# Conditional second scatters, shorter gathers and another row order of w_down in a 32-expert layer

## Chip, cores and metric

The kernel runs on one core of a Trainium2 chip. The metric is the device time of one execution in microseconds (us), lower is better.

## The reference

One decoder layer on x of shape 512 x 1024, float32: a mixing sublayer of three token mixers with an output projection and a LayerNorm, and then the part that this change touches, a routed feed-forward sublayer of 32 experts, of which each token uses 4:

```python
logits = (xt @ router_w + router_b).astype(F32)
top_val, top_idx = lax.top_k(logits, TOP_K)          # 4 of 32
gate = jax.nn.softmax(top_val, axis=-1)
...
gu = xb @ w_gu[e] + b_gu[e]                          # rows of expert e, 1024 x 2048
glu = jnp.minimum(gu[:, :D_FF], SWIGLU_LIMIT)
lin = jnp.clip(gu[:, D_FF:], -SWIGLU_LIMIT, SWIGLU_LIMIT)
act = glu * jax.nn.sigmoid(SWIGLU_ALPHA * glu) * (lin + 1.0)
return act @ w_dn[e] + b_dn[e]                       # 1024 x 1024
...
y_sorted = out[dest] * gate.reshape(-1)[order][:, None].astype(h.dtype)
y = jnp.zeros_like(xt).at[tok_sorted].add(y_sorted)
h = layer_norm(DEEPNORM_ALPHA * h + ffn, ln2_g[l], ln2_b[l])
```

So 512 x 4 = 2048 rows are spread over 32 experts, and each expert's weights (8 MB of w_gate_up and 4 MB of w_down in float32) are read once.

## The kernel before

The first 380 us hold the mixing sublayer. Then `experts` (line 1338) walks over the 32 experts. An expert has room for 96 slots (`CAP`); slots 0 to 63 are the low ones, 64 to 95 the high ones. Slots that no token fills are padding slots: their index in the table `gidx` points to one of 128 spare rows of zeros behind the 512 token rows of the DRAM buffer `hd`, and their row in `sidx` points to spare rows of the DRAM buffer `yd`.

For expert e the program does this:

- `load_gu` and `load_dn` (lines 1175 and 1183) issue eight loads of 1 MB of w_gate_up and four of 1 MB of w_down on SP's queue, through `load` (line 1171). They go into a ring of 18 buffers (`chunk`, tile `wc`), so a load waits until the load 18 places earlier has been used, and SP also waits for older loads to land. One partition of a w_gate_up load is one row of 8 KB; one partition of a w_down load is two rows of 4 KB that lie 128 rows apart.
- `expert_gather` (line 1191) issues on POOL an indirect DMA that reads 96 rows of 4 KB from `hd` into the tile `xg`, two experts ahead. `expert_xT` (line 1200) transposes them on PE (line 1206) and copies them with ACT.
- `gu_low` (line 1263) multiplies the low slots with w_gate_up, `gu_high` (line 1269) the high slots. The high part stands in a branch (`past64`, line 1256): `fill` (line 1249) reads the expert's count into a register of PE, and PE skips the part when the count is 64 or less. Experts 0 and 31 always take it.
- `swiglu` and `swiglu_T` (lines 1274 and 1287) apply the activation on DVE and ACT and transpose the result on PE in blocks of 128 columns.
- `dn` (line 1297) multiplies with w_down, one expert later: the low slots into the PSUM bank `p0`, the high slots into `p2`, these again in PE's branch. Then, for every expert but the last, ACT scales both banks with the gates (line 1329) and POOL issues two indirect DMAs that add into `yd` (line 1330): 128 rows of 2 KB for the low slots and 128 rows of 1 KB for the high slots, whether or not the high slots hold anything. The last expert's output goes another way, in `tail`.

A scheduler orders the instructions of each engine; a branch is moved only as a whole. After the last expert, `overflow` handles experts with more than 96 rows (a branch that is not taken here), and `tail` adds `yd` and applies the LayerNorm.

Of the kernel before, what the change touches and what calls it, by code (L numbers as in the profile page):

```python
# [24 lines left out]
F32 = mybir.dt.float32  # L25
# [4 lines left out]
AF = mybir.ActivationFunctionType  # L30
OP = mybir.AluOpType
# [4 lines left out]
T, D, NT, NK = 512, 1024, 4, 8  # L36
NE, FF = 32, 1024
KAPPA = math.exp(-0.5)
ALPHA = 2.0 ** 0.25
CAP = 96  # L40
# [86 lines left out]
class Trunk:  # L127
# [1055 lines left out]
    def load_dn(self, e):  # L1183
        out = []
        for k in range(0, NK, 2):
            w, gate = self.chunk()
            self.load(w.rearrange("p (k c) -> p k c", k=2), self.a["w_down"][e, k * 128:(k + 2) * 128].rearrange("(k p) c -> p k c", p=128), gate)
            out += [w[:, 0:1024], w[:, 1024:2048]]
        return out

    def expert_gather(self, e):
        x = self.mw.tile([128, D], F32, name="xg", bufs=2)
        self.nc.gpsimd.indirect_dma_start(out=x[0:CAP], out_offset=None, in_=self.hd,  # L1193
                                          in_offset=bass.IndirectOffsetOnAxis(ap=self.gidx[:, e:e + 1], axis=0))
        return x

    def tbank(self):
# [51 lines left out]
    def fill(self, e):  # L1249
        if e in (0, NE - 1):  # L1250
            return None
        return self.nc.values_load(self.cnti[0:1, e:e + 1], engines=[mybir.EngineType.PE], min_val=0, max_val=T,
                                   skip_runtime_bounds_check_because="a count of rows, which only decides a branch")


# [31 lines left out]
    def swiglu_T(self, t):  # L1287
        nc = self.nc
        aT = self.mw.tile([128, 6, 128], F32, name="aT")
        for z0, n in ((0, 4), (4, 2)):  # L1290
            p = self.tbank()
            for z in range(n):
                nc.tensor.transpose(p[:, z * 128:z * 128 + 128], t[:, (z0 + z) * 128:(z0 + z) * 128 + 128], self.ident)
            nc.scalar.activation(aT[:, z0:z0 + n], p[:, 0:128 * n].rearrange("p (z t) -> p z t", z=n), AF.Copy)  # L1294
        return aT

    def dn(self, e, aT, wd, n):
        nc, mm = self.nc, self.nc.tensor.matmul
        p0 = self.mps.tile([128, 512], F32, name="dn0")
        if e == 0:  # L1300
            self.dn2 = self.mps.tile([128, 512], F32, name="dn2")[:, 0:256]
        p2 = self.dn2

        def high():
            for k in range(NK):
                for c in range(4):
                    mm(p2[32 * c:32 * c + 32], aT[:, 4 + k % 2, 32 * (k // 2):32 * (k // 2) + 32], wd[k][:, 256 * c:256 * c + 256],  # L1307
                       start=(k == 0), stop=(k == NK - 1), skip_group_check=True)

        for k in range(NK):  # L1310
            for h in range(2):
                mm(p0[64 * h:64 * h + 64], aT[:, k % 4, 64 * (k // 4):64 * (k // 4) + 64], wd[k][:, 512 * h:512 * h + 512], start=(k == 0), stop=(k == NK - 1))  # L1312
        self.past64(n, high)
        if e == NE - 1:
            his = []
            for g, p in enumerate((p0, p2)):
                hi, lo = self.slast[2 * g:2 * g + 2]
                his.append(nc.scalar.activation(hi, p, AF.Copy, scale=self.gate[:, g, e:e + 1]))
                nc.vector.scalar_tensor_tensor(lo, p, self.gate[:, g, e:e + 1], hi, OP.mult, OP.subtract)
            self.warm = self.mw.tile([128, 1], F32, name="warm")  # L1320
            w = nc.scalar.activation(self.warm, self.eps[1e-5], AF.Sqrt)
            for h in his:
                self.after(w, h)
            return
        sts = []
        for g, p in enumerate((p0, p2)):
            n = 512 >> g
            o = self.mw.tile([128, n], F32, name=f"eo{g}")
            nc.scalar.activation(o, p, AF.Copy, scale=self.gate[:, g, e:e + 1])  # L1329
            sts.append(nc.gpsimd.indirect_dma_start(out=self.yd.rearrange("t (c f) -> (t c) f", f=n),  # L1330
                                                    out_offset=bass.IndirectOffsetOnAxis(ap=self.sidx[:, g, e:e + 1], axis=0),
                                                    in_=o, in_offset=None, compute_op=OP.add))
        self.tc.declare_no_dep(sts[1].ins, sts[0].ins, reason="rows of other slots")
        if self.added is not None:
            self.after(sts[1], self.added, mybir.DependencyClass.Sync)
        self.added = sts[0]

    def experts(self):
        xs, xT = {}, {0: self.first_xT()}
        wg, pend, self.added = self.load_gu(0), None, None  # L1340
        self.route_slots()
        for e in range(NE):
            w = wg
            t, sel = xT.pop(e)
            n = self.fill(e)
            p = self.gu(t, sel)
            for k in range(NK):
                self.gu_low(p, k, t, w[k])
                if k % 4 == 3:
                    self.past64(n, lambda: [self.gu_high(p, z, t, w[z]) for z in range(k - 3, k + 1)])  # L1350
                if e == 0:
                    if k == 0:
                        self.route_counts()
                        self.route_table()
                        self.tables()
                        xs[1] = self.expert_gather(1)
                    elif k < 5:
                        self.out_init(k - 1)
                if k == 3:
                    if e + 1 < NE:  # L1360
                        wg = self.load_gu(e + 1)
                    wd = self.load_dn(e)
                    if e + 2 < NE:
                        xs[e + 2] = self.expert_gather(e + 2)
                if k == (6 if e == 0 else 3) and e + 1 < NE:
                    xT[e + 1] = self.expert_xT(e + 1, xs.pop(e + 1))
            a = self.swiglu(p)
            if e == NE - 1:
                self.tail_setup()
                aT = self.swiglu_T(a)  # L1370
            if pend:
                self.dn(*pend)
            if e == NE - 1:
                self.tail_rows()
            pend = (e, aT if e == NE - 1 else self.swiglu_T(a), wd, n)
        self.dn(*pend)
# [290 lines left out]
```

## Time and profile before

| | us |
|---|---|
| median of 3 runs (lowest, highest) | 1513.34 (1508.01, 1516.6) |
| the profiled execution, its own time | 1505.45 |
| span of that execution, first to last instruction | 1503.7 |
| PE busy over the span | 1339.4 |
| DVE, ACT, POOL busy over the span | 464.9, 298.9, 251.3 |
| mean granted TensorE clock, as a share of full speed | 0.968 |

The profiled execution took 1.75 us more than its span. It is 0.5% below the median of the runs. "Busy" is the time in which an engine executes instructions; waits, branches and the issuing of DMAs are not in it. In the rows below an arrow names what ended an idle time, PEld is PE's loading of stationary operands, and q1 is the hardware queue of SP's loads, q0 the software queue of POOL's indirect DMAs.

### The profile page before, as it was taken

How to read it: one execution, taken by the hardware profiler on the slowest of the kernel's cores; microseconds unless marked ns; L12 is line 12 of the kernel's file. 1: busy time of each engine (PE TensorE's matmuls, PEld its weight loads, DVE VectorE, ACT ScalarE, POOL GpSimd, SP SyncE). 2: the span in 40 equal slices, each digit the busy share in tenths (PEclk: the TensorE clock that was granted, in tenths of full speed). 3: DMA queues.
4: the chain of work that ended last, by engine and by line, in shares of the span. 5: the costliest groups of instructions: out<-in, count | busy, mean ns of one | idle time of the engine just before them, and what ended most of it. 6: DMA issues, size and time to landing. Idle time of an engine off the chain costs nothing. (4 is left out here: it accounts for less than half of the span.)

```text
span 1503.7 us, 19610 instructions
## 1 busy us (share of the span) xinstructions
PE 1339.4 (89%) x7852; PEld 623.5 (41%) x7853; DVE 464.9 (31%) x1108; ACT 298.9 (20%) x628; POOL 251.3 (17%) x221
## 2 busy tenths in 40 slices
PE   7899979998899998987899999999888888899993
PEld 5577878875533432322223333333222222333322
DVE  4767687888621121111111121111111111111115
ACT  4444343443111111111111111111111110111103
POOL 1211227232201111111111111111111111110111
PEclk9999997999999999999999999999999999999996
DMA  7222233446699999999999999999999999999984
GB/s 252 65 56 70 49 75 101 140 143 236 251 377 393 382 392 392 392 387 387 395 393 395 393 394 395 394 388 393 390 388 395 395 396 394 395 394 406 401 284 131
DMA packets 114059, 467.94 MB, mean 311 GB/s; under 512 B 17412, under 2 KB 28196, under 8 KB 81178
## 3 DMA queue, kind: packets, MB, share of 16 engines
q1 hardware_dynamic: 96058, 434.57, 74.1%
q0 software_dynamic: 13328, 27.63, 8.3%
q10 hardware_dynamic: 4560, 4.15, 0.9%
q8 instruction: 82, 1.34, 0.4%
q14 instruction: 31, 0.25, 0.0%
HBM read 445.97 MB, written 20.33 MB: 310 GB/s over the span
## 5 line engine op out<-in xcount | busy, mean ns | idle before, releaser
L1267 PE MATMUL gu<-wc,xT 128*64 128x512 f32 x2048 | 491.4, 608 | 85.6 <-DMA wc<-w_gate_up 82.8
L1267 PEld LDWEIGHTS gu<-wc,xT 128*64 128x64 f32 x2048 | 140.3, 138 | 420.0 <-issue 233.0
L1280 DVE TENSOR_SCALAR glu<-gu 128x256 f32<-128x256 f32 (+1 forms) x64 | 35.6, 556 | 865.3 <-PEq L1260 398.6
L1312 PE MATMUL dn<-wc,aT 128*64 128x512 f32 x1024 | 247.7, 603 | 3.5 <-PEq L1260 2.1
L1281 ACT ACTIVATE glu<-glu 128x256 f32<-128x256 f32 (+1 forms) x64 | 33.5, 524 | 574.0 <-DVE glu L1280 573.8
L1193 POOL DMA_INDIRECT xg<-hd,gidx x31 | 29.5, 952 | 668.9 <-PE tr L1206 656.4
L1330 POOL DMA_INDIRECT yd<-eo,sidx x62 | 96.4, 1555 | 267.6 <-ACT eo L1329 267.1
L1312 PEld LDWEIGHTS dn<-wc,aT 128*64 128x64 f32 x1024 | 65.5, 136 | 117.3 <-issue 101.6
L1272 PE MATMUL gu<-wc,xT 128*32 128x512 f32 x960 | 111.3, 596 | 0.0
L222 PE MATMUL pi<-xhi,whi 128*128 128x512 f32 x152 | 63.4, 417 | 8.8 <-ACT whi L172 8.8
L1329 ACT ACTIVATE eo<-dn,gate 128x512 f32<-128x512 f32 (+1 forms) x62 | 36.0, 581 | 167.7 <-PE dn L1307 78.1
L223 PE MATMUL pi<-xlo,whi 128*128 128x512 f32 x152 | 63.0, 414 | 0.8 <-DVE xlo L173 0.6
L1207 ACT ACTIVATE xT<-tr 128x384 f32<-128x384 f32 x62 | 29.9, 491 | 167.0 <-PE tr L1206 167.0
L173 POOL TENSOR_TENSOR wlo<-wraw,whi 128x512 fp32r<-128x512 f32 (+1 forms) x28 | 39.8, 1425 | 135.0 <-ACT whi L172 132.4
L224 PE MATMUL pi<-xhi,wlo 128*128 128x512 f32 x152 | 61.1, 402 | 0.0
L1272 PEld LDWEIGHTS gu<-wc,xT 128*32 128x32 f32 x960 | 27.7, 109 | 79.2 <-issue 79.2
L1307 PE MATMUL dn<-wc,aT 128*32 128x256 f32 x960 | 56.1, 381 | 1.0 <-ACT aT L1294 1.0
L172 ACT ACTIVATE whi<-wraw 128x512 fp32r<-128x512 f32 (+1 forms) x54 | 33.9, 631 | 54.1 <-DMA wraw<-w_in 27.0
L1307 PEld LDWEIGHTS dn<-wc,aT 128*32 128x32 f32 x960 | 29.5, 110 | 33.4 <-issue 14.0
L1283 DVE SCALAR_TENSOR_TENSOR glu<-glu 128x256 f32<-128x256 f32 (+1 forms) x64 | 35.6, 556 | 7.7 <-ACT glu L1281 6.9
L222 PEld LDWEIGHTS pi<-xhi,whi 128*128 128x128 f32 x152 | 29.4, 193 | 18.1 <-ACT whi L172 8.5
L1282 DVE TENSOR_SCALAR glu<-gu 128x256 f32<-128x256 f32 (+1 forms) x64 | 35.3, 551 | 3.0 <-PE gu L1267 3.0
(488 smaller groups left out, 1544.0 us busy)
## 6 DMA issues: line engine op xcount, KB each, us to landing
wc<-w_gate_up SPq DMA_DIRECT2D x256, 1024.0 KB
wc<-w_down SPq DMA_DIRECT2D x128, 1024.0 KB
wraw<-w_in SPq DMA_DIRECT2D x46, 256.0 KB
wraw<-w_out SPq DMA_DIRECT2D x16, 256.0 KB
xraw<-xT SPq DMA_DIRECT2D x4, 512.0 KB
res<-x SPq DMA_DIRECT2D x4, 512.0 KB
hd<-res ACTq DMA_DIRECT2D x4, 512.0 KB
res<-yd POOLq DMA_DIRECT2D x4, 512.0 KB
```

What stands on the lines that cost most here:

```text
L173: return (eng or nc.vector).tensor_tensor(lo, src, hi, OP.subtract)
L222: nc.tensor.matmul(p, hi, xh, start=(k == 0), stop=False)
L223: nc.tensor.matmul(p, hi, xl, start=False, stop=False)
L224: nc.tensor.matmul(p, lo, xh, start=False, stop=(k == NK - 1))
L1267: mm(p[q][64 * h:64 * h + 64], xT[:, k, 0:64], w[:, 1024 * q + 512 * h:1024 * q + 512 * h + 512], start=False, stop=(k == NK - 1))
L1272: self.nc.tensor.matmul(p[2][32 * c:32 * c + 32], xT[:, k, 64:96], w4[:, c], start=False, stop=(k == NK - 1), skip_group_check=True)
L1280: nc.vector.tensor_scalar(out[:, c], g, 7.0, None, OP.min)
L1283: nc.vector.scalar_tensor_tensor(out[:, c], ln[:, c], 1.0, out[:, c], OP.add, OP.mult)
L1307: mm(p2[32 * c:32 * c + 32], aT[:, 4 + k % 2, 32 * (k // 2):32 * (k // 2) + 32], wd[k][:, 256 * c:256 * c + 256], start=(k == 0), stop=(k ...
L1312: mm(p0[64 * h:64 * h + 64], aT[:, k % 4, 64 * (k // 4):64 * (k // 4) + 64], wd[k][:, 512 * h:512 * h + 512], start=(k == 0), stop=(k == N ...
L1329: nc.scalar.activation(o, p, AF.Copy, scale=self.gate[:, g, e:e + 1])
L1330: sts.append(nc.gpsimd.indirect_dma_start(out=self.yd.rearrange("t (c f) -> (t c) f", f=n), out_offset=bass.IndirectOffsetOnAxis(ap=self.s ...
```

## The change

Three things change. The low slots' output is scaled and scattered as soon as the low matmuls are done; the scaling and the scatter of the high slots move into the branch that holds their matmuls, so the count is now loaded into registers of ACT and POOL too, and these two engines branch as PE does. The gather gets a bounds check: indices over 511, which are those of the padding slots, are not fetched, so `xg` becomes two fixed tiles that are set to zero once at the start of `experts`. And a load of w_down puts two neighbouring rows (8 KB in one piece) in one partition; to match, the transposes after SwiGLU take every second column of a block of 256 instead of 128 neighbouring columns.

```diff
--- before.py
+++ after.py
@@ -1184,14 +1184,15 @@
         out = []
         for k in range(0, NK, 2):
             w, gate = self.chunk()
-            self.load(w.rearrange("p (k c) -> p k c", k=2), self.a["w_down"][e, k * 128:(k + 2) * 128].rearrange("(k p) c -> p k c", p=128), gate)
+            self.load(w.rearrange("p (k c) -> p k c", k=2), self.a["w_down"][e, k * 128:(k + 2) * 128].rearrange("(p k) c -> p k c", k=2), gate)
             out += [w[:, 0:1024], w[:, 1024:2048]]
         return out
 
     def expert_gather(self, e):
-        x = self.mw.tile([128, D], F32, name="xg", bufs=2)
+        x = self.xg[e % 2]
         self.nc.gpsimd.indirect_dma_start(out=x[0:CAP], out_offset=None, in_=self.hd,
-                                          in_offset=bass.IndirectOffsetOnAxis(ap=self.gidx[:, e:e + 1], axis=0))
+                                          in_offset=bass.IndirectOffsetOnAxis(ap=self.gidx[:, e:e + 1], axis=0),
+                                          bounds_check=T - 1, oob_is_err=False)
         return x
 
     def tbank(self):
@@ -1249,7 +1250,7 @@
     def fill(self, e):
         if e in (0, NE - 1):
             return None
-        return self.nc.values_load(self.cnti[0:1, e:e + 1], engines=[mybir.EngineType.PE], min_val=0, max_val=T,
+        return self.nc.values_load(self.cnti[0:1, e:e + 1], engines=[mybir.EngineType.PE, mybir.EngineType.Activation, mybir.EngineType.Pool], min_val=0, max_val=T,
                                    skip_runtime_bounds_check_because="a count of rows, which only decides a branch")
 
 
@@ -1287,10 +1288,11 @@
     def swiglu_T(self, t):
         nc = self.nc
         aT = self.mw.tile([128, 6, 128], F32, name="aT")
+        t2 = t.rearrange("q (c p z) -> q c z p", z=2, p=128)
         for z0, n in ((0, 4), (4, 2)):
             p = self.tbank()
             for z in range(n):
-                nc.tensor.transpose(p[:, z * 128:z * 128 + 128], t[:, (z0 + z) * 128:(z0 + z) * 128 + 128], self.ident)
+                nc.tensor.transpose(p[:, z * 128:z * 128 + 128], t2[:, (z0 + z) // 2, z % 2], self.ident)
             nc.scalar.activation(aT[:, z0:z0 + n], p[:, 0:128 * n].rearrange("p (z t) -> p z t", z=n), AF.Copy)
         return aT
 
@@ -1310,7 +1312,28 @@
         for k in range(NK):
             for h in range(2):
                 mm(p0[64 * h:64 * h + 64], aT[:, k % 4, 64 * (k // 4):64 * (k // 4) + 64], wd[k][:, 512 * h:512 * h + 512], start=(k == 0), stop=(k == NK - 1))
-        self.past64(n, high)
+        def out(g, p):
+            w = 512 >> g
+            o = self.mw.tile([128, w], F32, name=f"eo{g}")
+            nc.scalar.activation(o, p, AF.Copy, scale=self.gate[:, g, e:e + 1])
+            return nc.gpsimd.indirect_dma_start(out=self.yd.rearrange("t (c f) -> (t c) f", f=w),
+                                                out_offset=bass.IndirectOffsetOnAxis(ap=self.sidx[:, g, e:e + 1], axis=0),
+                                                in_=o, in_offset=None, compute_op=OP.add)
+
+        if e < NE - 1:
+            first = out(0, p0)
+
+        def past():
+            high()
+            if e < NE - 1:
+                second = out(1, p2)
+                self.tc.declare_no_dep(second.ins, first.ins, reason="rows of other slots")
+                if self.added is not None:
+                    self.after(second, self.added, mybir.DependencyClass.Sync)
+
+        self.past64(n, past)
+        if e < NE - 1:
+            self.added = first
         if e == NE - 1:
             his = []
             for g, p in enumerate((p0, p2)):
@@ -1321,21 +1344,11 @@
             w = nc.scalar.activation(self.warm, self.eps[1e-5], AF.Sqrt)
             for h in his:
                 self.after(w, h)
-            return
-        sts = []
-        for g, p in enumerate((p0, p2)):
-            n = 512 >> g
-            o = self.mw.tile([128, n], F32, name=f"eo{g}")
-            nc.scalar.activation(o, p, AF.Copy, scale=self.gate[:, g, e:e + 1])
-            sts.append(nc.gpsimd.indirect_dma_start(out=self.yd.rearrange("t (c f) -> (t c) f", f=n),
-                                                    out_offset=bass.IndirectOffsetOnAxis(ap=self.sidx[:, g, e:e + 1], axis=0),
-                                                    in_=o, in_offset=None, compute_op=OP.add))
-        self.tc.declare_no_dep(sts[1].ins, sts[0].ins, reason="rows of other slots")
-        if self.added is not None:
-            self.after(sts[1], self.added, mybir.DependencyClass.Sync)
-        self.added = sts[0]
 
     def experts(self):
+        self.xg = [self.mw.tile([128, D], F32, name=f"xg{q}") for q in range(2)]
+        for x in self.xg:
+            self.nc.gpsimd.memset(x[0:CAP], 0.0)
         xs, xT = {}, {0: self.first_xT()}
         wg, pend, self.added = self.load_gu(0), None, None
         self.route_slots()
```

## Rows read from the trace of the kernel before

**Rows 1.** The page's slices: what the DMA engines moved, 40 slices of 37.6 us

```profile
GB/s 252 65 56 70 49 75 101 140 143 236 251 377 393 382 392 392 392 387 387 395 393 395 393 394 395 394 388 393 390 388 395 395 396 394 395 394 406 401 284 131
```

**Rows 2.** Windows, three stretches: length, busy (instructions) of each engine, PEclk, DMA share, GB/s

```profile
434.00:570.00 136.00, 134.53 (x758) 51.87 (x756) 21.01 (x46) 20.07 (x41) 20.90 (x16) 1.00 1.03 390
570.00:1318.00 748.00, 664.59 (x3718) 218.28 (x3718) 94.37 (x220) 85.08 (x172) 86.64 (x65) 0.99 1.03 393
1318.00:1454.00 136.00, 132.41 (x824) 42.61 (x813) 19.32 (x40) 14.33 (x29) 14.08 (x10) 1.00 1.01 392
```

**Rows 3.** Waits of PE, 570 to 1318 us: total, times, longest

```profile
PE gu L1267 <- DMA wc<-w_gate_up: 79.7, 84, 2.7
```

**Rows 4.** Timeline of SP's queue: start, length, loads of w_gate_up; first and last periods

```profile
579.34 18.25 SPq L1171 DMA_DIRECT2D wc<-w_gate_up  x8
...
1334.18 17.94 SPq L1171 DMA_DIRECT2D wc<-w_gate_up  x8
...
1366.13 18.07 SPq L1171 DMA_DIRECT2D wc<-w_gate_up  x8
```

**Rows 5.** Windows of 6 and 3.5 us: weights alone, then beside a gather

```profile
1106.00:1112.00 6.00, 5.78 (x32) 2.36 (x30) 0.00 (x0) 1.01 (x3) 0.95 (x1) 1.00 1.02 418
1114.20:1117.70 3.50, 1.94 (x8) 0.48 (x8) 0.00 (x0) 1.45 (x3) 1.62 (x2) 1.00 1.04 318
```

**Rows 6.** DMA queues in 1114.2:1117.7 (gather): packets, MB, share of 16 engines

```profile
q1 hardware_dynamic: 100, 0.72, 67.3%
q0 software_dynamic: 93, 0.38, 34.7%
q8 instruction: 1, 0.02, 2.1%
```

**Rows 7.** DMA queues in 1118.4:1121.6, the scatter of 1 KB rows

```profile
q1 hardware_dynamic: 136, 1.00, 78.0%
q0 software_dynamic: 133, 0.13, 25.5%
```

**Rows 8.** DMA queues in 1121.6:1125.6, the scatter of 2 KB rows

```profile
q1 hardware_dynamic: 159, 1.16, 71.4%
q0 software_dynamic: 157, 0.26, 35.8%
```

**Rows 9.** DMA packets in 690:694 (w_down alone) and in 1352:1360 (w_gate_up alone)

```profile
DMA packets 430, 1.64 MB, mean 410 GB/s; under 512 B 30, under 2 KB 30, under 8 KB 430
...
DMA packets 460, 3.36 MB, mean 420 GB/s; under 512 B 51, under 2 KB 51, under 8 KB 51
```

**Rows 10.** The page's groups: the experts' matmuls, two instructions for each call

```profile
L1267 PE MATMUL gu<-wc,xT 128*64 128x512 f32 x2048 | 491.4, 608 | 85.6 <-DMA wc<-w_gate_up 82.8
...
L1272 PE MATMUL gu<-wc,xT 128*32 128x512 f32 x960 | 111.3, 596 | 0.0
...
L1307 PE MATMUL dn<-wc,aT 128*32 128x256 f32 x960 | 56.1, 381 | 1.0 <-ACT aT L1294 1.0
```

**Rows 11.** Lines 1260 and 1252, PE's sequencer: duration ns min/median/max, first and last start

```profile
L1260 PEldq COMPARE_BRANCH  x129: 65/179/369, 426.4 to 1448.3; - x129
...
L1252 PEldq TENSOR_LOAD <-cnti x30: 297/306/482, 425.8 to 1393.2; - x30
```

**Rows 12.** Timeline of POOL: one expert's gather and scatters, idle time before each

```profile
1110.19 0.95 POOL L1193 DMA_INDIRECT xg<-hd,gidx  x1 [24.82 <-PE tr L1206]
1112.72 1.56 POOL L1330 DMA_INDIRECT yd<-eo,sidx  x1 [1.58 <-ACT eo L1329]
1115.17 1.55 POOL L1330 DMA_INDIRECT yd<-eo,sidx  x1 [0.90 <-ACT eo L1329]
1147.69 0.95 POOL L1193 DMA_INDIRECT xg<-hd,gidx  x1 [30.97 <-PE tr L1206]
```

**Rows 13.** Line 1293, the transposes after SwiGLU: duration ns min/median/max

```profile
L1293 PEld LDWEIGHTS tr<-ident,glu x192: 137/140/143, 424.8 to 1448.0; 128*128 128x128 f32 x192
```

**Rows 14.** POOL around the start of the experts: groups, and its timeline

```profile
L688 POOL MEMSET ba<- 96x1024 f32 x1 | 0.9, 948 | 8.1 <-PE ps L652 8.1
...
391.84 2.58 POOL L1097 TENSOR_TENSOR ohv<-ohv,ro 128x512 f32<-128x512 f32 x1 [9.13 <-DVE ohv L1098]
```

## The prediction

> **What bounds the kernel now.** I read the page's slices first: from the twelfth slice to the thirty-eighth the DMA engines move 377 to 406 GB/s without a break [rows 1], and this is the walk over the experts. Then I asked for windows of that stage. In three stretches of four, twenty-two and four experts the DMA share is 1.03, 1.03 and 1.01, so the sixteen engines are never idle; PE is busy for 134.5 of 136 us, 664.6 of 748 us and 132.4 of 136 us [rows 2]. So in the middle stretch PE has 748 - 664.6 = 83.4 us of idle time, and the waits name its cause: 79.7 us for loads of w_gate_up [rows 3]. In the first and last stretch the two are nearly in balance, with 1.5 and 3.6 us of PE idle. The reader is to see that the DMA engines set the pace of the middle stretch, that a microsecond taken from their work there is a microsecond of the kernel until PE's idle time is used up, and that at both ends PE leaves little to win.
>
> One period is seen in SP's timeline: 22 experts from 579.34 to 1334.18 us, 34.3 us each; the next, which holds no gather since the last expert's rows are already there, takes 1366.13 - 1334.18 = 31.95 us [rows 4]. An expert's weights are 12 MB in units of 1,048,576 bytes, 12.58 million bytes; at the 418 GB/s of undisturbed weights [rows 5] they need 30.1 us. So the gather and the two scatters cost about 4.2 us of DMA time per expert, 1.9 us of it scatters and 2.4 us the gather.
>
> **The change part by part.** DMA time first, as a loss: the length of a window, less the time that the weights moved in it would need alone.
>
> Gather: in 3.5 us only 0.72 + 0.02 million bytes of weights and instructions move [rows 6], 1.77 us worth at 418, so it costs 1.73 us. The share stays at 1.04 while the rate falls to 318 GB/s [rows 5], so no engine waits: the packets get slower, those of the weights too. The gather's own packets take 34.7% of 3.5 us, 1.21 us; the other 0.5 us is slowing of its neighbours. Of 31 x 96 = 2976 gathered rows, 2048 less expert 0's own (65 to 96, as it takes the branch with no row beyond 96) are real, so a third is padding. No row of this trace shows a gather with rows left out. The saving per gather lies between nothing (if the skipped rows, which stand together at the end, belong to a few of the sixteen engines while the others carry theirs as before; a load has landed only when its slowest part has) and a third of the 2.4 us that the periods give, 0.8 us. I take a third of the packets' own time, 0.40 us, since that time is what the row shows to belong to the rows themselves.
>
> Scatter of the high slots: 3.2 us with 1.00 million bytes of weights, 2.39 us worth, so 0.81 us [rows 7]; its packets' time, 25.5% of 3.2, is 0.82 us too. (The low slots' scatter costs 4 - 1.16 / 0.418 = 1.22 us by [rows 8]; the three together are 3.8 us beside the 4.2 us of the periods.) How many vanish: the low gate-up matmuls are 2048 for 32 experts, 64 each; the high ones are 960, again 64 for each expert that takes the branch, so 15 do, experts 0 and 31 among them [rows 10], and 17 skip both matmuls now and scatter in the future. By the order of PE's branches 12 of the 17 scatters fall in the middle stretch, 3 before it and 2 after.
>
> w_down: where it is alone on the engines they move 410 GB/s, where w_gate_up is alone 420 GB/s [rows 9]. 4.19 million bytes take 10.23 and 9.99 us, so 8 KB rows save 0.24 us per expert; the lower bound is nothing, since mixed stretches run at 418. I take 0.24. The Trainium skill, "DMA: Bandwidth & Descriptors", section "Why small descriptors are slow (HBM only)", gives each packet a fixed overhead of about 3 cycles beside one for each 32 bytes: worked out from its figures, an estimate of 131 against 129.5 cycles for 4 KB, 1.1%, or 0.11 us per expert. Our rows show 2.4%; by the page the forecast would be 3 us later, so nothing hangs on it.
>
> What is added. ACT and POOL load a count and branch for 30 experts. PE does so already: 0.31 us for a load, 0.18 us at the median and 0.37 us at most for a branch [rows 11]. I cost it at nothing, because POOL idles 25 to 31 us before each gather [rows 12] and ACT is busy for 85 of 748 us [rows 2]; uncovered it would be 30 x 0.5 = 15 us. On ACT the scaling of the high slots now waits inside the branch for PE's high matmuls, with the next copies to `xT` and `aT` queued behind it; on POOL the scatter waits for that scaling, with the gather two experts ahead behind it. The gather has a whole period in hand, so neither moves PE unless the order on ACT changes (a rival below). The low scatter leaves a few us earlier, which changes no amount of DMA work. The transposes now load every second column: a load takes 140 ns [rows 13]; the bounds are 0 and double that, 192 x 0.14 = 27 us of PE over the stage if none of it overlapped; I take 0, since loads run beside matmuls, and the middle stretch would cover its share, 18 us, in PE's idle time. The bounds check lengthens a POOL instruction at most, in the same idle time. Setting `xg` to zero is twice the 0.95 us of a 96 x 1024 memset, in the 9.1 us that POOL waits before line 1097 [rows 14]; it may disturb DVE's routing there, bounds 0 and 2 us, and I take 1 us. Skipping ACT's scaling 17 times frees an engine that bounds nothing.
>
> **The sum.** Middle stretch: 12 x 0.81 + 22 x 0.40 + 22 x 0.24 = 9.7 + 8.8 + 5.3 = 23.8 us, well below PE's 83.4 us of idle. First stretch: 3 x 0.81 + 4 x 0.40 + 4 x 0.24 = 5.0 us less DMA work, of which I count PE's idle 1.5 us. Last stretch: 2 x 0.81 + 4 x 0.24 = 2.6 us, within PE's 3.6 us. Less 1 us for the start: 23.8 + 1.5 + 2.6 - 1 = 26.9 us, say 27. Against the profiled execution 1505.45 - 27 = 1478.4 us. The runs' median lies 7.9 us above that execution, so for the median I forecast 1513.3 - 27 = 1486 us.
>
> **The rivals.** (1) The skipped rows and the longer rows save nothing: only the scatters count, 27 - 8.8 - 5.3 = 13 us, 1500 us. For it: the weights' packets suffer beside a gather as long as any engine still carries it. Against it: packets' own time falls with their number. (2) The gather's cost falls by a full third of what the periods show: 22 x 0.4 = 9 us more, 1477 us, and still within PE's idle time. (3) PE takes over as the bound, by added work or waits of d us per expert: the transposes' loads double without overlap (27 / 32 = 0.85 us), and ACT's branch holds copies up. The middle stretch hides 22 d up to 83 - 24 = 59 us, the eight experts at the ends hide nothing. At 0.85 us 7 us are lost and 20 us of gain remain; at 2.5 us, 20 us, and the time is 1506 us, no change that can be told. (4) Slower: the branch blocks of ACT, the same sum with a larger d. Were the copies to `xT` ordered behind the block, PE would stand between two experts until the high matmuls and the scaling are done and the copies made, or until the skip is signalled. The price is at most the 56.1 / 15 = 3.7 us of high matmuls [rows 10] and two copies, some 4 to 5 us per expert. At 3 us the middle loses 66 - 59 = 7 and the ends 24 us, 1517 us; so it decides from about 3 us, and at 4 us it gives 1486 + 29 + 32 = 1547 us. Against it: PE has branched so all along, and the copies to `xT` need the transposes alone, not the scaling. The Trainium skill, "Runtime: NRT & Kernel Launch", section "Instruction fetch mechanics", says that a taken branch out of the prefetched window stalls on a fetch, which would feed this rival; 129 branches on PE with none above 0.37 us [rows 11] do not show it.
>
> **How the numbers follow.** The forecast's case, 20 to 34 us gained, gets 0.50; rival 1, 10 to 20 us, 0.20; rival 2, above 34 us, 0.10; rival 3 with a gain under 8 us, 0.12; rival 4, 0.08. A measurement of this kernel can tell about 0.5%, 7.6 us, from no change. So faster 0.80, same 0.12, slower 0.08. The range: all terms at their upper bounds give 1470 us (22 x 0.4 = 9 us for the gather, 3.5 us of the first stretch's lost gain and 1 us at the start, with 2 us for the runs' own spread), the lower ones 27 - 14 - 1 for the start - 3 for transposes at the ends = 9 us of gain, 1504 us. 1470 to 1504 us leaves out about 2 in 10, mostly rivals 3 and 4.
>
> **What would show it.** In the profile after: 45 instead of 62 scatters; some 990 fewer packets of 4 KB in the software queue, and w_down's 8 KB packets; periods of about 33 us; windows beside a gather that are shorter, not just emptier; the DMA share still about 1.03 in the middle stretch with PE idle near 60 us. The prediction is wrong if that share falls below 1 (PE or a wait has taken over), if PE's waits name ACT's copies or branches, or if a gather still costs 1.7 us.

## The result and the profile after

The changed kernel takes 1492.94 us (median of 4 runs, 1488.69 to 1493.81), the kernel before 1511.91 us on the same chip (one run more than the three ahead of the prediction); the ratio is 0.9878 [0.9855, 0.9901], 18 to 19 us less. The profiled execution took 1492.41 us with a span of 1490.7 us, 13.0 us below the span of before.

Windows of the middle and the last stretch of the changed kernel, as in [rows 2] (length, busy time of PE, PEld, DVE, ACT and POOL, granted clock, DMA share, GB/s):

```profile
570.00:1318.00 748.00, 680.77 (x3850) 230.22 (x3850) 94.39 (x220) 83.28 (x168) 74.64 (x56) 0.99 1.02 396
...
1318.00:1454.00 136.00, 132.97 (x820) 43.15 (x812) 19.37 (x41) 13.60 (x27) 14.59 (x13) 1.00 0.92 356
```

PE's idle time in the middle fell from 83.4 to 67.2 us, and its waits there still name one cause, as in [rows 3]:

```profile
PE gu L1268 <- DMA wc<-w_gate_up: 62.9, 72, 2.9
```

SP's timeline, the issues that answer to [rows 4] (start, length, work):

```profile
581.86 18.79 SPq L1171 DMA_DIRECT2D wc<-w_gate_up  x8
...
1321.63 17.99 SPq L1171 DMA_DIRECT2D wc<-w_gate_up  x8
1351.93 18.70 SPq L1171 DMA_DIRECT2D wc<-w_gate_up  x8
```

The same 22 experts take 1321.63 - 581.86 = 739.8 us, where they took 754.8; a period is 33.6 us instead of 34.3. So the middle stretch gave 15.1 us. It begins 2.5 us later than before, and from its end to the end of the kernel 169.1 us pass, where 169.5 did.

The page's packets and queues (packets, MB, share of sixteen engines):

```profile
DMA packets 95232, 461.67 MB, mean 310 GB/s; under 512 B 18137, under 2 KB 26745, under 8 KB 45962
...
q1 hardware_dynamic: 79674, 434.57, 74.1%
q0 software_dynamic: 10880, 21.32, 6.6%
```

The skipped rows are still there. The promised sign was some 990 fewer packets of 4 KB in the software queue beside the 17 absent scatters; the bytes fell so, but the number of packets did not: a later run that fetches all rows has the same 10880 packets with 25.40 MB, and 997 fewer of all packets are under 512 bytes (17140 against 18137). So a skipped row is still a packet, of a few bytes. Of the other signs, 45 scatters are left as forecast, and the periods are 33.6 us instead of about 33.

The added work, lines 1261 and 1295, answering to [rows 11] and [rows 13] (duration ns min/median/max, first and last start):

```profile
L1261 POOLq COMPARE_BRANCH  x129: 34/40/57, 427.0 to 1409.7; - x129
L1261 ACTq COMPARE_BRANCH  x129: 34/40/50, 433.1 to 1432.3; - x129
L1261 POOLq INC_SWDGE_SEM  x17: 338/1015/1675, 462.9 to 1409.9; - x17
...
L1295 PEld LDWEIGHTS tr<-ident,glu x192: 194/209/219, 431.8 to 1435.0; 128*128 128x128 f32 x192
```

POOL's timeline at the start of the experts, answering to [rows 14]:

```profile
380.05 4.58 POOL L1012 TENSOR_TENSOR res<-res,ln 128x512 f32<-128x512 f32 x3 [6.36 <-DVE lmv L1003]
...
387.25 1.84 POOL L1351 MEMSET xg<- 96x1024 f32 x2
398.85 2.58 POOL L1097 TENSOR_TENSOR ohv<-ohv,ro 128x512 f32<-128x512 f32 x1 [9.77 <-DVE ohv L1098]
```

Line 1012 is work that the change does not touch; before it stood at 375.46 us. From there to line 1097 it was 16.4 us and is 18.8. DVE's cast takes 1.86 us beside the memsets, where it took 0.16 us before (below, first the kernel before, then the changed one), and PE's wait for `sel` grew from 2.3 to 4.0 us.

```profile
382.66 0.16 DVE L1052 CAST ro<-i 128x4 f32<-128x4 uint32 x1
```

```profile
387.25 1.86 DVE L1052 CAST ro<-i 128x4 f32<-128x4 uint32 x1
```

The two profiled spans, cut at these marks, against the terms of the forecast:

| stretch | forecast, us | measured, us |
|---|---|---|
| up to line 1012, unchanged work | 0 | +4.6 |
| line 1012 to line 1097 (memsets) | +1 | +2.4 |
| line 1097 to the first of the 22 periods | -1.5 | -4.5 |
| 22 periods | -23.8 | -15.1 |
| from there to the end | -2.6 | -0.4 |
| sum | -26.9 | -13.0 |

Two things ask for an explanation: the 8.7 us that are missing in the middle, and the start.

### The profile page after: what moved, and what is told of

Its sections match the earlier page's. It is cut to its first block, busy times and chain, and to the rows that moved or that the text cites. A ratio compares the mean times of both kernels' runs of the same rounds, so it can differ in the third digit from the quotient of the medians.

```text
span 1490.7 us, 19988 instructions
## 1 busy us (share of the span) xinstructions
PE 1345.4 (90%) x7852; PEld 639.2 (43%) x7853; DVE 466.6 (31%) x1108; ACT 290.7 (20%) x611; POOL 228.2 (15%) x206
## 2 busy tenths in 40 slices
DMA packets 95232, 461.67 MB, mean 310 GB/s; under 512 B 18137, under 2 KB 26745, under 8 KB 45962
## 3 DMA queue, kind: packets, MB, share of 16 engines
q0 software_dynamic: 10880, 21.32, 6.6%
## 5 line engine op out<-in xcount | busy, mean ns | idle before, releaser
L1281 DVE TENSOR_SCALAR glu<-gu 128x256 f32<-128x256 f32 (+1 forms) x64 | 35.6, 556 | 843.8 <-PE gu L1273 391.5
L1282 ACT ACTIVATE glu<-glu 128x256 f32<-128x256 f32 (+1 forms) x64 | 33.6, 525 | 549.6 <-DVE glu L1281 549.4
L1319 POOL DMA_INDIRECT yd<-eo,sidx x45 | 70.1, 1557 | 276.1 <-ACT eo L1318 276.1
L1318 ACT ACTIVATE eo<-dn,gate 128x512 f32<-128x512 f32 (+1 forms) x45 | 28.0, 621 | 162.9 <-PE dn L1314 84.4
L172 ACT ACTIVATE whi<-wraw 128x512 fp32r<-128x512 f32 (+1 forms) x54 | 33.9, 631 | 56.4 <-DMA wraw<-w_in 25.3
L1295 PEld LDWEIGHTS tr<-ident,glu 128*128 128x128 f32 x192 | 25.7, 208 | 28.0 <-DVE sel L1214 19.5
```

Source lines behind the costliest of these rows:

```text
L172: self.hi_ins = nc.scalar.activation(hi, src, AF.Copy)
L1281: nc.vector.tensor_scalar(out[:, c], g, 7.0, None, OP.min)
L1319: return nc.gpsimd.indirect_dma_start(out=self.yd.rearrange("t (c f) -> (t c) f", f=w), out_offset=bass.IndirectOffsetOnAxis(ap=self.sidx[ ...
```

## The experiments

The edits below are shortened, partly to words; each run is against the kernel before unless another is named. "22 periods" is read as above from SP's timeline of the one profiled execution. Two kernels that moved the same bytes differ there by 2.7 us (740.7 and 743.4 us, below), so a few us of such a sum cannot be told from nothing; the medians of several runs carry the verdicts.

| kernel | 22 periods, us | against before | median, us | ratio to before |
|---|---|---|---|---|
| before | 754.8 | | 1509 to 1512 | 1 |
| changed | 739.8 | -15.1 | 1492.94 | 0.9878 [0.9855, 0.9901] |
| scatter alone | 747.5 | -7.4 | 1498.97 | 0.9929 [0.9904, 0.9953] |
| gather alone | 752.0 | -2.9 | 1508.59 | 0.9990 [0.9975, 1.0004] |
| w_down alone | 748.8 | -6.0 | 1503.58 | 0.9955 [0.9942, 0.9969] |
| scatter and w_down | 740.7 | -14.1 | 1491.46 | 0.9878 [0.9853, 0.9904] |
| changed, no memset | 738.9 | -15.9 | 1489.99 | 0.9861 [0.9833, 0.9889] |
| changed, slots dealt out | 730.7 | -24.2 | 1478.08 | 0.9786 [0.9764, 0.9808] |
| slots dealt out, all rows fetched | 743.4 | -11.5 | 1491.75 | 0.9874 [0.9853, 0.9895] |
| slots dealt out, no memset | 730.3 | -24.6 | 1476.05 | 0.9770 [0.9748, 0.9792] |
| the same, scatters skip padding too | 729.3 | -25.6 | 1471.32 | 0.9747 [0.9722, 0.9772] |
| before without high matmuls | 751.4 | -3.4 | 1505.80 | 0.9969 [0.9952, 0.9986] |
| changed without high matmuls | 735.8 | -19.0 | 1480.52 | 0.9817 [0.9783, 0.9850] |

**One part at a time.** The theory: every saving of DMA work in the middle stretch counts, and the forecast mis-sized a term. The rival: some parts save nothing. Scatter alone:

```diff
-engines=[PE]
+engines=[PE, Activation, Pool]
...
-self.past64(n, high)          # both scalings and scatters follow
+first = out(0, p0)
+self.past64(n, past)          # past: high(), then out(1, p2)
```

> The kernel before, with the scatter of the high slots put into the branch and nothing else. Theory A (every saving of DMA work counts): 12 x 0.81 us in the middle stretch, about 1.5 us in the last, little in the first, so 10 to 12 us less than before. Theory B (rival 1 of the prediction: the scatters alone bring the whole gain): 17 to 19 us less. Theory C (the branch on ACT and POOL costs time): less than 8 us saved, with waits of PE that name ACT.

Measured: 12.0 us less in medians, 10.7 by the ratio, 7.4 of it in the 22 periods. Theory A; no wait of PE for ACT takes its place, so C falls.

Gather alone:

```diff
-x = self.mw.tile([128, D], F32, name="xg", bufs=2)
+x = self.xg[e % 2]            # two fixed tiles, set to zero once
 indirect_dma_start(out=x[0:CAP], ..., gidx[:, e:e + 1]
+                   , bounds_check=T - 1, oob_is_err=False)
```

> The kernel before, with the bounds check of the gather, its two fixed tiles and the memset, and nothing else. Theory A: the loss beside a gather fell from 1.86 to 1.50 us in the changed kernel, so 22 x 0.36 = 8 us saved in the middle, about 2 us given back at the start beside the memsets, 5 to 8 us less than before in all. Theory B (skipped rows save nothing, since the other engines carry theirs as before): 0 to 2 us more than before.

Measured: 1.5 us less by the ratio, whose interval holds 1. It lies between the two theories and nearer to B: 22 gathers save 2.9 us, 0.13 us each, within what two executions differ by. The 0.36 us of the expectation was a mean over windows beside the gathers, in which the bytes of all sixteen engines are added; it overstated what PE gets.

w_down alone:

```diff
-w_down[e, rows].rearrange("(k p) c -> p k c", p=128)
+w_down[e, rows].rearrange("(p k) c -> p k c", k=2)
...
-transpose(p[...], t[:, (z0 + z) * 128:(z0 + z) * 128 + 128], ident)
+transpose(p[...], t2[:, (z0 + z) // 2, z % 2], ident)
```

> The kernel before, with w_down read two rows to a partition and the transposes that answer to it, and nothing else. Theory A: 22 x 0.24 = 5 us saved in the middle stretch, perhaps 1 us given back by the slower strided loads at the ends, 4 to 6 us less than before. Theory B (longer rows save nothing, the strided loads cost): 0 to 3 us more than before.

Measured: 6.8 us less by the ratio, 6.0 in the 22 periods, 0.27 us per expert. Theory A, a little above it. By the ratios the three parts make 10.7 + 1.5 + 6.8 = 19.0 us; together they make 18.4. The parts add up, and the gather brings almost nothing.

**The whole without the gather's part.**

> The kernel before with the scatter in the branch and the new reading of w_down, without the gather's part. Theory A (the gather's part is worth 1.5 to 4 us in the whole): 15 to 17 us less than before, 22 periods of about 741.5 us together. Theory B (the fixed tiles of xg bring a later start, as the three runs with them show 4.6 to 5.9 us at POOL's line 1012): 19 us less than before or more, and POOL's line 1012 stands at 375 to 376 us.

Measured: the same ratio as the changed kernel, 0.9878. So the gather's part is worth nothing in the whole, memsets included: less than A expected. B's cause falls too: this kernel has no fixed tiles of `xg`, and yet its line 1012 stands at 379.07 us. What goes with a late line 1012 is the granted TensorE clock (the third number from the right) in unchanged work at 172 to 194 us. Windows of that stretch, first the changed kernel:

```profile
172.00:194.00 22.00, 22.00 (x115) 20.41 (x115) 10.47 (x27) 3.20 (x10) 3.73 (x6) 0.62 0.23 49
```

then scatter and w_down, without the fixed tiles:

```profile
172.00:194.00 22.00, 22.00 (x119) 20.63 (x119) 10.39 (x27) 3.20 (x10) 3.73 (x6) 0.64 0.20 40
```

and the kernel before:

```profile
172.00:194.00 22.00, 21.94 (x175) 20.53 (x176) 15.69 (x35) 7.73 (x25) 6.43 (x8) 1.00 0.34 76
```

Of the thirteen profiled executions eight have 0.61 to 0.64 there and line 1012 at 378.9 to 382.4 us; five have 1.00 and line 1012 at 375.5 to 378.7 us. Kernels with and without the fixed tiles are in both groups, and the runs of the kernel before differ by themselves, from 1504.78 us at a mean clock of 0.973 to 1512.79 us at 0.960. The 4.6 us at the start of the changed kernel are therefore, in the main, variation of the mixing stage from execution to execution, which the medians average. (A smaller share of the tiles is not excluded: at a clock of 1.00 the two kernels with them stand at 378.4 and 378.7 us, the three without at 375.5 to 376.1.) Without these 4.6 us the two spans differ by 17.6 us, close to the medians.

**Without the memset.**

```diff
-for x in self.xg: memset(x[0:CAP], 0.0)
...
-bounds_check=T - 1, oob_is_err=False)
+**({} if e < 3 else dict(bounds_check=T - 1, oob_is_err=False)))
```

> The changed kernel without the two memsets of xg: the gathers for experts 1 and 2 fetch all their 96 rows without a bounds check, so that the padding rows bring the zeros. Theory A (the memset on POOL slows DVE's casts and holds up the start): DVE's cast of sel takes 0.16 us again, PE waits 2.3 us for sel, and the kernel takes about 2 us less than the changed one, 20 to 21 us less than before. Theory B (the later start of the changed kernel's profiled execution was variation of the stages ahead of it): no change, 18 to 19 us less than before.

Measured: 2.9 us below the changed kernel by the medians, 2.6 by the ratios, line 1012 to line 1097 back at 16.3 us, the cast at 0.16 us and PE's wait for `sel` at 2.3 us. Theory A for what the memsets do to DVE and PE; how much of the whole time they cost is less sure, since the intervals of the two ratios overlap. The late line 1012 stayed, at 381.33 us.

**Does PE take what the DMA engines save?** Both kernels without the matmuls of the high slots:

```diff
-if k % 4 == 3:
+if k % 4 == 3 and n is None:       # experts 0 and 31 only
     self.past64(n, ... gu_high ...)
...
-high()
+if n is None:
+    high()
```

> The kernel before without the matmuls of the high slots for experts 1 to 30 (this work is left out; the scatters and all loads stay). It is the base for the next run. Theory A (DMA work alone sets the middle stretch): within 5 us of the kernel before there, with more idle time of PE. Theory B (PE bounds the periods of the experts past 64): 8 us or more below before.

> The changed kernel without the matmuls of the high slots for experts 1 to 30 (this work is left out, the scatters stand where the change put them). Against the base without these matmuls: Theory A (what the forecast lacks was never saved as DMA work): 22 periods about 15 us shorter, as with the matmuls. Theory B (DMA work fell by the 23.8 us of the forecast and PE ate the rest): 22 to 25 us shorter.

Measured: the base stands 3.4 us below the kernel before in the 22 periods, its theory A. The changed kernel's 22 periods are 15.6 us shorter than the base's, beside 15.1 with the matmuls. Theory A: the missing 8.7 us were never saved as DMA work, and PE did not take them in the middle. The medians differ by 25.3 us, B's number, but not for B's reason: of 30.2 us between the two spans 3.5 are the start up to line 1012, and the ends give the rest. From the last of the 22 periods to the end 170.3 us became 164.4, 5.9 us less, where the change with the matmuls had 0.4. Windows of the last stretch, the base and then the changed kernel without the high matmuls, show that PE has room there now.

```profile
1318.00:1454.00 136.00, 115.58 (x526) 32.93 (x522) 19.47 (x38) 13.41 (x28) 13.91 (x10) 0.99 1.03 402
```

```profile
1318.00:1454.00 136.00, 113.56 (x566) 36.42 (x563) 20.61 (x41) 14.69 (x29) 14.57 (x13) 0.97 0.94 353
```

With the matmuls PE is busy for 133.0 of 136 us (the window above). The DMA share of 0.92 there is no sign of it, since it is 0.94 without the matmuls too: the loads end inside the window. When they end tells more. Windows of 2 us, first the kernel before, then the changed one:

```profile
1446.00:1448.00 2.00, 2.00 (x8) 0.69 (x8) 1.86 (x6) 0.00 (x0) 0.00 (x0) 1.00 1.03 414
1448.00:1450.00 2.00, 2.00 (x10) 0.74 (x12) 2.00 (x5) 0.00 (x0) 0.00 (x0) 1.00 0.73 287
```

```profile
1428.00:1430.00 2.00, 2.00 (x16) 0.48 (x8) 0.41 (x1) 0.00 (x0) 0.00 (x0) 1.00 1.00 418
1430.00:1432.00 2.00, 2.00 (x14) 0.49 (x13) 1.73 (x4) 0.63 (x1) 0.00 (x0) 1.00 0.70 291
```

The DMA share falls 113.8 us after the start of the last of the 22 periods before, and 108.4 us after it in the changed kernel, but from there to the end 55.7 us pass before and 60.7 us after. So the loads are done 5 us sooner, and PE, busy throughout these windows, does not follow: PE is the bound at the end, and what the DMA engines save there is lost.

**Where the skipped rows stand.** The padding slots are the last of the 96. If each DMA engine takes a block of six consecutive rows, an expert with 64 rows leaves ten engines with all six, one with four and five with none. Dealing the slots out gives each engine four:

```diff
+pid = ident[0:96, 0:96] with column 6j+i taken from column 16i+j
-tensor_copy(self.gidx, self.tt[:, 0:32])
+matmul(p[0:CAP, 256:288], self.pid, self.tt[:, 0:32])
+tensor_copy(self.gidx, p[0:CAP, 256:288])
...
-activation(xT[...], p.rearrange("p (k t) -> p k t", k=4), Copy)
+activation(xT[...] as "p k (i j) -> p k i j", p as "p (k j i) -> p k i j", Copy)
```

> The changed kernel with the gathered slots dealt out in another order: partition 6j+i of xg holds slot 16i+j, so that the skipped slots at the end of the 96 stand on all partitions' blocks of six alike; ACT puts the columns of xT back in order when it copies them. So far the skipping saved 2.9 us over 22 periods where it stands alone, 0.13 us per gather. Theory A (each DMA engine takes a block of consecutive rows, the skipped rows belong to a few engines and the others carry all six of theirs): the loss beside a gather falls by another 0.2 to 0.3 us, 4 to 7 us less in the middle stretch than the changed kernel, 22 to 26 us less than before in all. Theory B (a row skipped costs a packet all the same, wherever it stands): no change, 18 to 19 us less than before, or a few us worse by the copies in four runs of columns.

Measured: 1478.08 us, 31 us below before in medians and 32 by the ratio. Theory A, and more than it expected: the 22 periods are 9.1 us shorter than those of the changed kernel and 10.0 shorter than without the gather's part. SP's timeline of this kernel:

```profile
576.75 20.09 SPq L1175 DMA_DIRECT2D wc<-w_gate_up  x8
...
1307.43 18.34 SPq L1175 DMA_DIRECT2D wc<-w_gate_up  x8
```

The packets show the difference. DMA in windows of 0.5 us in the changed kernel, early and late in one gather (q0 is the gather):

```profile
DMA packets 71, 0.16 MB, mean 312 GB/s; under 512 B 48, under 2 KB 48, under 8 KB 56
...
q0 software_dynamic: 47, 0.03, 23.4%
...
DMA packets 28, 0.18 MB, mean 352 GB/s; under 512 B 3, under 2 KB 3, under 8 KB 10
...
q0 software_dynamic: 10, 0.03, 18.5%
```

At 1108.89 us 47 packets pass with 0.03 MB, so most of them are skipped rows, while the real rows have hardly begun; two us later, at 1110.89, real rows still come, seven packets of 4 KB among the ten of the queue in 0.5 us. With the slots dealt out, at 1097.53 and 1099.53 us of another gather:

```profile
DMA packets 27, 0.14 MB, mean 279 GB/s; under 512 B 3, under 2 KB 3, under 8 KB 17
...
q0 software_dynamic: 14, 0.06, 39.8%
...
DMA packets 52, 0.19 MB, mean 377 GB/s; under 512 B 29, under 2 KB 29, under 8 KB 29
...
q0 software_dynamic: 26, 0.00, 3.7%
```

Now the real rows come together first, at a share of 39.8%, and the skipped ones last, 26 packets with 0.00 MB at 3.7%.

**Is it the order or the skipping?**

```diff
 # slots dealt out as above, no memset
-bounds_check=T - 1, oob_is_err=False)
```

> The kernel with the slots dealt out in the other order, but with all 96 rows gathered again (no bounds check, no memset of xg). It tells the order of the slots from the skipping. Theory A (the order only matters because it divides the skipped rows evenly among the engines): without skipping the gain of the order is gone; the 22 periods come back to the 740.7 us of the kernel with the scatter and w_down alone, 17 to 20 us less than before in all. Theory B (the order of the rows itself makes the gather cheaper): 22 periods near 731 us, about 30 us less than before.

Measured: 743.4 us for 22 periods, ratio 0.9874. Theory A: the order alone brings nothing, the skipping alone next to nothing, both together 10 to 13 us in the 22 periods. SP's timeline, and the page's packets with the gather's queue:

```profile
579.80 18.73 SPq L1175 DMA_DIRECT2D wc<-w_gate_up  x8
...
1323.17 17.83 SPq L1175 DMA_DIRECT2D wc<-w_gate_up  x8
```

```profile
DMA packets 95232, 465.75 MB, mean 312 GB/s; under 512 B 17140, under 2 KB 25748, under 8 KB 45962
...
q0 software_dynamic: 10880, 25.40, 7.4%
```

**Two steps further.** The same order without the memsets, and then a bounds check in the scatters (`bounds_check=(T << (1 + g)) - 1`):

> The kernel with the slots dealt out in the other order, without the memsets; the gathers for experts 1 and 2 fetch all 96 rows. Theory A (the memsets cost about 2 us, as they did without the new order): 1475 to 1477 us, 32 to 34 us less than before. Theory B (their cost goes under in the variation of the start): 1478 us as with them.

> The kernel of the run before, with a bounds check in the scatters too, so that the rows of padding slots are not added. These rows stand at the end of each block of 64 or 32 partitions, not dealt out. Some 450 padding slots are left in the scatters that still run; at 1.22 us for 64 slots and 0.81 us for 32 (the losses read in the kernel before) they are worth 8 to 11 us if each skipped row saved its share. Theory A (an engine takes a block of consecutive rows, and the fullest engine counts): most of that is not had, 0 to 3 us less than the kernel without it. Theory B (each skipped row saves its share wherever it stands): 8 us less or more.

Measured: without the memsets 1476.05 us, as A expected, though 2.0 us is within the spread of the runs. With the scatters' check the queue moves 1.9 MB less, 461 slots of 4 KB, near the 450 expected; the 22 periods are 1.0 us shorter, which is A's range. The medians differ by 4.7 us, above A and below B; 3.5 us of the difference in the profiled spans (4.7 us too) is the earlier line 1012, so whether more than about 1 us belongs to the scatters stays open. This is the fastest of these kernels, about 2.5% below before and 1.3% below the changed one.

## Why the prediction was right, and where it was not

The time, 1493 us, lies within 1470 to 1504 us and is 7 us above the forecast. By the gain, though, it is in the band of rival 1 (10 to 20 us), not in the forecast's (20 to 34): the range was wide enough to hold a sum of which one term failed.

- **The bound of the middle stretch** was read rightly. The DMA share stays above 1, PE waits for w_gate_up, three savings of DMA work add up, and removing PE's high matmuls from both kernels leaves the difference at 15.6 us.
- **The gather, 8.8 us in the middle, is the step that failed.** The prediction named the bounds, nothing "if the skipped rows, which stand together at the end, belong to a few of the sixteen engines", and 0.8 us, and took 0.40 us. The lower bound held: 2.9 us alone, 0.9 us beside the other parts (739.8 against 740.7), 0.13 and 0.04 us per gather, so the gather still costs nearly what it did, which the prediction had named as a sign of being wrong. With the slots dealt out the term comes to (740.7 - 730.7) / 22 = 0.45 us per gather, and the middle sum to 24.2 us, where 23.8 was forecast: the price was right, the condition was not met. That each engine has a block of consecutive rows is inferred from the packets in time; that the place of the skipped rows decides is shown by the runs. The Trainium skill, "DMA: Bandwidth & Descriptors", section "Why a DMA increments its semaphore by 16 and not by 1", says that a transfer over 96 partitions is shared among sixteen engines, and that all of them must have finished before it has landed. These runs agree with it: 0.04 us saved per gather with the skipped rows together, 0.45 us with them dealt out. No trace here shows the engines one by one.
- **Rival 1** was half right: skipped rows save next to nothing, but longer rows do save.
- **w_down**, 0.24 us per expert, measured 0.27 in the 22 periods. Over the whole run the ratio gives 6.8 us, with an interval of 4.7 to 8.8. The estimate of 0.11 us that the prediction works out from the Trainium skill's figures for the overhead of a packet ("DMA: Bandwidth & Descriptors", section "Why small descriptors are slow (HBM only)") would make it 32 x 0.11 = 3.5 us, less than was measured.
- **The scatter**, 9.7 us in the middle, measured 7.4, 0.62 us each instead of 0.81, in one execution; the difference of 2.3 us is within what two executions differ by (w_down alone against both together gives 748.8 - 740.7 = 8.1 us). Over the whole run it brought 10.7 us by the ratio.
- **The ends.** Of the 2.6 us of the last stretch 0.4 came, because PE took over there; the 3.6 us of idle time that the prediction meant to use were not all to be had. The first stretch gave 4.5 us instead of 1.5, after a later start; how much of that is a start caught up again stays open.
- **Costed at nothing** and found so: the branches, 40 ns at the median on ACT and POOL with no wait of PE behind them. That speaks against rivals 3 and 4. The Trainium skill, "Runtime: NRT & Kernel Launch", section "Instruction fetch mechanics", says that a taken branch out of the prefetched window stalls on a fetch; no branch here shows such a stall (57 ns at most on ACT and POOL), and no run tells whether one left the window. The strided loads of the transposes rose from 140 to 209 ns, 192 x 0.069 = 13 us of PEld; w_down alone shows the full gain all the same, so they are covered.
- **The memsets**, taken as 1 us of at most 2, lengthened the way from line 1012 to line 1097 by 2.4 us in this profiled execution, but by only 0.9 to 1.0 us in the three other profiled kernels that have them (17.3 to 17.4 us against 16.4). The medians put them at 2 to 3 us, within overlapping intervals, so the 1 us is not shown to be wrong.
- **Expert 0's rows** were put at 65 to 96 because it takes the branch, but it takes it at any count. The third that was taken for the padding is right all the same: 997 of 2976 rows are skipped.

## What to carry to other kernels

Leaving rows out of the gather paid only once the rows left out were dealt evenly over the partitions, 0.45 us per gather against 0.04, and then it paid its full share. A transfer that is over when its fullest engine is done would behave so. For the scatters it stays open. Price a saving by the resource that sets the pace in that stretch, and check the stretches at both ends separately, for a saving of DMA work counted next to nothing at the end, where PE is the bound. Cut two profiled spans at marks in unchanged work before reading small differences: here 4.6 us of them belonged, in the main, to no part of the change.

## What the runs showed of the hardware that was not expected

- A row that the bounds check leaves out stays a packet in the queue: 10880 packets with and without skipping, 21.32 against 25.40 MB, and 997 more packets under 512 bytes.
- A skipped scatter is not free on POOL: 17 semaphore instructions of 1.0 us at the median stand in its place. They stand in POOL's idle time.
- Loading every second column of a float32 tile into PE takes 209 ns instead of 140.
- A cast of 128 x 4 on DVE takes 1.86 us beside the memsets on POOL and 0.16 us without them. POOL's work of line 1012 does so too: beside it line 1052's cast at 377.60 us takes 1.23 us in the kernel before.
- The granted clock of one unchanged stretch of 22 us is 1.00 in some executions and 0.61 to 0.64 in others; in the changed kernel it stood at 0.50, the lower of the two levels of 2.4 and 1.2 GHz, from 172 to 188 us. Ahead of it PE did the same in that kernel and in the one before: busy for 4.00, 4.00 and 3.43 us in the three windows of 4 us from 160 us, at a full clock up to 168 us.
